# Weight tiles split into exact parts whole instead of in halves, in a two-block model's kernel

## The chip, the cores and the metric

The kernel runs on one core of a Trainium2 chip. The metric is the device time in microseconds of one execution. A profile of one execution lies beside the timed runs; its engines are named PE (TensorE's matmuls), PEld (TensorE's loads of the stationary operand), DVE (VectorE), ACT (ScalarE), POOL (GpSimd) and SP (SyncE, which issues most transfers).

## The reference: two model blocks in float32

The input is one sequence of 256 tokens of 1024 values, and a memory of 256 tokens. Block 1 is a token mixer (stick-breaking attention and a gated delta rule in chunks of 64), a cross attention to the memory, and a layer of product-key experts; block 2 is a second token mixer (gated linear attention and a spatial gating unit) and a second layer of experts. Each part is a norm, some dense layers `y = x @ w`, and something between them. The experts, which hold most of the weights, are

```python
def peer(xn, w_pq, subkeys, peer_u, peer_v):
    q = (xt @ w_pq).reshape(T, PEER_HEADS, 2, PEER_QDIM // 2)
    s = jnp.einsum('thpd,hpnd->thpn', q, subkeys)
    ...  # the 16 best of 128 x 128 sums of two scores per head: expert, gate
    def block(args):
        act = jax.nn.gelu(jnp.einsum('thkd,td->thk', peer_u[eb], xb), approximate=False) * gb
        return jnp.einsum('thk,thkd->td', act, peer_v[eb])
```

There are 16384 experts in each of the two layers. The kernel does not gather them: it multiplies every token with all rows of `peer_u` (the first layer of the experts), multiplies the activations by a dense matrix of gates that is zero where an expert was not chosen, and multiplies the result with all of `peer_v` (the second layer).

## The kernel before, in words

**Weights.** All weights come from memory in tiles of 128 x 1024 float32 values (512 KB). `load` (line 277) takes one of four `raw` buffers and issues the transfer from SP. `weight` (line 282) makes the two exact parts of a tile: `wh`, the values rounded to TensorE's float32r, and `wl`, what is left. Each part is made as two halves of 512 columns, with ScalarE's copy at line 274 for `wh` and VectorE's subtraction at line 275 for `wl`, both in `split`:

```python
    def split(self, hi, lo, src):
        self.nc.scalar.activation(hi, src, AF.Copy)
        self.nc.vector.tensor_tensor(lo, src, hi.bitcast(F32), ALU.subtract)
...
        raw = self.early.pop() if self.early else self.load(ap)
        wh, wl = [], []
        for i in range(2):
            wh.append(self.pw.tile([128, 512], F32R, tag="wh", bufs=HALF, name="wh"))
            wl.append(self.pw.tile([128, 512], F32R, tag="wl", bufs=HALF, name="wl"))
            self.split(wh[i], wl[i], raw[:, 512 * i:512 * i + 512])
        return Blocks(wh), Blocks(wl)
```

`HALF` is 7: there are seven half-size buffers for `wh` and seven for `wl`, so three and a half tiles. A half is written again when the matmuls that read it are done. The class `Blocks` gives the k-th block of 128 columns, or a whole half.

**Matmuls.** Each product is the sum of three: high by high, high by low and low by high (`mm3`, line 298, and the loops at lines 339 and 1265). In `dense` (line 301) a tile holds 128 output columns for all 1024 inputs, its eight blocks of 128 columns are the stationary operands in order, the tokens are the moving one (256 columns), and a tile takes 24 matmuls, twelve on each half. In `dense_tok` (line 326) and in the second layer of the experts (line 1265, `acc`) the half itself is the moving operand (512 columns); a tile takes twelve matmuls, six on the first half and then six on the second.

**Stages.** `mixer1`, `cross`, `peer`, `between`, `mixer2`, `peer`, `finish`, one after the other. In the mixers, `mix` weaves a chain of dependent steps (for instance `gdn`, the gated delta rule, with the triangular inverse by blocks of doubling size) with dense layers. In `peer` it weaves the selection of the experts (`route`, `gates`: sorting instructions and one-hot matrices on VectorE) with the first layer (`up`, `ph` in the profile). What is left of the first layer alternates with tiles of the second, and then the second layer goes on alone. For the second layer `prep` multiplies four rows of activations `hid` by gates `gt` that come by DMA (line 1209, VectorE) and splits the product into `dah` and `dal` (lines 274 and 275, ScalarE and VectorE).

**Order.** The tile framework puts the instructions of each engine into one order when the program is built, from the program's order and its own estimates of when operands and buffers are there. On the chip each engine takes its instructions strictly in that order, and waits where one is not ready.

There are 694 weight tiles in all, 512 of them in the two layers of experts.

Of the kernel before, what the change touches and what calls it, by code (L numbers as in the profile page):

```python
# [7 lines left out]
F32R = mybir.dt.float32r  # L8
# [10 lines left out]
T = 256  # L19
# [8 lines left out]
# pairs (a, b) of ranks that can be among the 16 best sums of two descending lists of 16: (a + 1) * (b + 1) <= 16, in  # L28
# the order of a * 16 + b; runs of equal length: first a, how many, length
RUNS = [(0, 1, 16), (1, 1, 8), (2, 1, 5), (3, 1, 4), (4, 1, 3), (5, 3, 2), (8, 8, 1)]  # L30
NC = 50
# blocks of q (0-3), k and v of the gated delta rule, in the order of their use
# [3 lines left out]
# ---------------------------------------------------------------- host layout  # L36
def _cols(w):
    """[K, C] -> [C/128, 128 p, K/128, 128 c]: one stationary tile per 128 columns."""
    k, c = w.shape
    return np.ascontiguousarray(w.reshape(k // 128, 128, c // 128, 128).transpose(2, 1, 0, 3))  # L40


def _rows(w):
    """[K, 512] -> [K/256, 128 p, 2, 512]: moving tiles, two blocks of 128 rows each."""
    k, c = w.shape
    return np.ascontiguousarray(w.reshape(k // 256, 2, 128, c).transpose(0, 2, 1, 3))


def _vec(v):
    """[n*128] -> [128, n]"""  # L50
    return np.ascontiguousarray(v.reshape(-1, 128).T)
# [107 lines left out]
# ---------------------------------------------------------------- the program  # L159
class Vec:  # L160
    """[128, n, 256] kept as tiles of four blocks"""
# [8 lines left out]
class Blocks:  # L170
    """[128, 1024] kept as two halves; [k] is the k-th block of 128 columns"""

    def __init__(self, half):
        self.half = half

    def __getitem__(self, k):
        return self.half[k // 4][:, k % 4 * 128:k % 4 * 128 + 128]
# [12 lines left out]
def weave(a, b):  # L190
    """steps of a and b by turns"""
    for _ in a:
        yield _
        v = next(b, None)
        if v is not None:
            yield v
    yield from b


def mix(a, b):  # L200
    """Two programs in one order. A step yields the vector engine's time that it takes, less what it leaves
    while the tensor engine is busy with it; a runs on what b leaves."""
# [16 lines left out]
class Norm:  # L219
    """x * g in exact halves (act), and the tokens' 1 / rms apart from it: rc with tokens on partitions, rb as rows.  # L220
    The latter are made when they are first asked for."""
# [12 lines left out]
class Net:  # L234
# [21 lines left out]
    # -- tiles  # L256
# [15 lines left out]
    # -- exact halves of float32: hi rounded to the tensor engine's float32r, lo the rest  # L272
# [9 lines left out]
    def weight(self, ap):  # L282
        """a tile [128, 1024] from memory: its exact parts, each as two halves"""
        raw = self.early.pop() if self.early else self.load(ap)
        wh, wl = [], []
        for i in range(2):
            wh.append(self.pw.tile([128, 512], F32R, tag="wh", bufs=HALF, name="wh"))
            wl.append(self.pw.tile([128, 512], F32R, tag="wl", bufs=HALF, name="wl"))
            self.split(wh[i], wl[i], raw[:, 512 * i:512 * i + 512])
        return Blocks(wh), Blocks(wl)  # L290

    def mm3(self, out, pairs):
        """sum of (ah+al)^T (bh+bl), without al^T bl, which is under float32's last place"""
# [7 lines left out]
    def dense(self, w, n, act, use):  # L301
        """w: tiles of 128 columns with K = 1024; use(pair, psum[128 c, 2 * 256 t])"""
# [11 lines left out]
    def dense_half(self, w, n, act, use):  # L314
        """w: tiles of two blocks of 128 columns with K = 512"""
# [10 lines left out]
    def dense_tok(self, w, act, use):  # L326
        """tokens on partitions: out[t, 512]; w: four moving tiles of two blocks of 128 rows; use(th, psum)"""
# [17 lines left out]
    def rsqrt(self, y, v, name):  # L345
        """y = v ** -0.5 for v > 0 on a few columns: a first value from the exponent, three Newton steps"""
# [14 lines left out]
    def spread(self, cols, n, out=None):  # L361
        """cols [128 t, n] -> the columns as rows on every partition: psum tiles of four [128, 128 t] each"""
# [12 lines left out]
    def begin(self, x, g, name, stats=True):  # L375
        """the norm of x[k] [128, 256] times g [128, 8], whose pairs of blocks are yet to be fed"""
# [51 lines left out]
    def colsum(self, ps, c, n, x):  # L428
        """ps[:, c] of n columns: the sums of x [128, 128 t] over its partitions"""
# [7 lines left out]
    def copies(self, v, N, scale=1.0):  # L437
        """use() that keeps pairs of column tiles in a Vec, times the tokens' 1 / rms"""
# [25 lines left out]
    def tables(self, which):  # L464
        """the activation tables that the calls of fn() after this one use, loaded after those before it are done"""
# [18 lines left out]
    # ------------------------------------------------------------ block 1, token mixer  # L484
    def sb_attention(self, qk, v, o):
        """stick-breaking; qk: Vec of 8 (4 of q / 8, 4 of k), two heads each; v [t][128, 512]; o: exact halves"""
# [4 lines left out]
        # scores, keys on partitions: of the first 128 keys all queries, of the others the last 128  # L491
# [17 lines left out]
        # softplus, which is zero where masked, and its sums over a key and those after it  # L509
# [24 lines left out]
    def gdn(self, pads, z, ba, out, ready):  # L534
        """gated delta rule; pads: 4 tiles [128, 3, 259] of q, k, v with three columns of zeros first;
        z [128 t, 2, 512]; ba [128 t, 2, 8] (b, then a); out: exact halves, Vecs of 4. ready: names of the blocks
        of pads, of ba and of z as they get there"""
# [17 lines left out]
        # beta, g, and the cumulative sums of g within chunks of 64  # L555
# [22 lines left out]
        gf = g.rearrange("p h c -> p (h c)")  # pack = 2 * head + half  # L578
# [13 lines left out]
        # l2 norms over the head's 128 partitions: k now, q with the output  # L592
# [18 lines left out]
        dm = self.big("dm", (8, 128))   # exp(gc_i - gc_j), i on partitions  # L611
        dt = self.big("dt", (8, 128))   # the same with j on partitions
        eg = self.big("eg", (8, 128))   # exp(gc) on every partition
# [8 lines left out]
        # of the differences d = gc_free - gc_partition only the signs that a causal pair can have  # L622
# [8 lines left out]
        # A, and q k^T with m on partitions  # L631
# [13 lines left out]
        # (I + A)^-1 by blocks of doubling size; Tm the inverse, P its transpose  # L645
# [11 lines left out]
        for s in (2, 4, 8, 16, 32):  # L657
# [25 lines left out]
            if s == 2:  # L683
                # meanwhile k and v with tokens on partitions, and q exp(gc)
# [14 lines left out]
        # u [c, dv] and w^T [dk, c]  # L699
# [11 lines left out]
        # the scan over chunks  # L711
# [38 lines left out]
    def head_out(self, po, th, z, g, out, rq=None, half=False):  # L750
        """the exact halves of rmsnorm(po * rq) * z * g for the heads' [128 t, 128], transposed; half: with z / 2"""
# [31 lines left out]
    def branches(self, gates, wa, oa, wb, ob, wout, N):  # L783
        """N: the norm of the new x.  x += (sigmoid(ga) * (oa @ wa) + sigmoid(gb) * (ob @ wb)) @ wout; gates: Vec of 16;
        sigmoid(y) = (tanh(y / 2) + 1) / 2"""
# [27 lines left out]
    def add_x(self, N):  # L813
        """use() that adds to x and feeds x's next norm"""
# [75 lines left out]
    # ------------------------------------------------------------ cross attention  # L890
# [23 lines left out]
    def patterns(self):  # L914
        """constants of the experts' selection, in 16 bits, which hold them"""
# [8 lines left out]
    def cross(self, N, kv):  # L924
# [54 lines left out]
        # the values of the last two heads, while the tensor engine has little else to do  # L979
# [10 lines left out]
    # ------------------------------------------------------------ product-key experts  # L990
    def peer(self, N, g, wpq, sub, shared, u, v, gelu, final):
        """returns psum tiles acc[t half][d half] of [128 t, 512] with x plus the experts' sums, and the tile of the
        final gain in rows"""
# [13 lines left out]
        # scores of half the heads and half the tokens each; later the gates on their way to memory  # L1007
# [11 lines left out]
        def scores():  # L1019
            """of the last head asked for; the tensor engine meanwhile has the next one's tiles"""  # L1020
# [14 lines left out]
        # of each selected expert: its two indices, and its gate times 2^15 in two parts of 11 bits  # L1035
# [4 lines left out]
        def route(hq, th):  # L1040
# [27 lines left out]
            # 64 * the first index + the place of the run, as steps from run to run  # L1068
# [41 lines left out]
            # the second index by its rank  # L1110
# [30 lines left out]
        def gates():  # L1141
            for t0 in range(0, T, 4):
# [3 lines left out]
                # one-hots of the first index; of the second, times each part of the gate  # L1146
# [54 lines left out]
        def prep(i0):  # L1201
            """gated activations of four rows of the table, in exact halves"""
# [29 lines left out]
        # the filler may reach the expert tables only after the normalized x is there  # L1232
# [5 lines left out]
        def tokens():  # L1238
            """adds x"""
# [9 lines left out]
        for i0 in range(0, 128, 4):  # L1249
# [3 lines left out]
            for i in range(4):  # L1253
                w[i] = self.weight(v[i0 + i])
                # the last two tiles go through the tokens' halves one after the other
# [11 lines left out]
                # what is left of the first layer, as the second one frees its place  # L1267
# [9 lines left out]
    def between(self, acc, gf):  # L1277
        """x <- rmsnorm(x + sums, g_final), and the next norm of it"""
# [26 lines left out]
        # the means of x^2 and (x g_final)^2, with eps; of the latter as the next norm has it, by the squared first rms  # L1305
# [48 lines left out]
    # ------------------------------------------------------------ block 2, token mixer  # L1354
    def mixer2(self, N):
# [5 lines left out]
        # the low rank and, on its own partition, a one for the bias  # L1361
# [168 lines left out]


class Rows:
    """the blocks of a [128, 8, 256] tile or Vec"""

    def __init__(self, x):
        self.x = x
# [31 lines left out]
```

## Time and profile before

| what | value |
|---|---|
| median of 3 runs | 2252.29 us (2251.95 to 2252.83) |
| span of the profiled execution | 2251.2 us |
| TensorE, matmuls | 2230.4 us busy, 99% of the span |
| VectorE | 1643.0 us, 73% |
| ScalarE | 1229.7 us, 55% |
| granted clock of TensorE, mean | 0.997 |
| read from memory, written | 403.89 MB, 34.60 MB |

The time of the profiled execution is its span; what lies around it is the 1.1 us to the runs' median. Busy time is the union of an engine's instructions. A matmul that waits for its operands can count as busy, so the numbers of matmuls in a stretch say more than its busy share. In a line of the page, `wl<-raw,wh 128x512 fp32r<-128x512 f32 x1388` is what an instruction writes and reads, its shapes and how often it ran; what stands in brackets or behind a bar is the idle time ahead of it and what ended that.

### The profile page before, as it was taken

The page shows a single profiled execution, that of the slowest core. Times are in us where ns is not written, and L with a number is a line of the kernel's source. Part 1 is how long each engine was busy: PE and PEld are TensorE (multiplying, and loading weights), DVE is VectorE, ACT ScalarE, POOL GpSimd, SP SyncE. Part 2 cuts the span into 40 slices and gives each one's busy share as a digit, 9 for nine tenths or more (in the row PEclk, how much of TensorE's full clock was granted, in tenths as well). Part 3 has the DMA queues.
Part 4 walks back from the last instruction along what each step waited for, and adds up shares of the span by engine and source line. Part 5 has one row for each costly group of instructions (what it writes and reads, how often), then busy time and mean ns, then how long its engine had stood idle before and what let it go on. Part 6 is the DMA issues. An engine that isn't in the chain of part 4 may idle for free.

```text
span 2251.2 us, 40741 instructions
## 1 busy us (share of the span) xinstructions
PE 2230.4 (99%) x15268; PEld 2035.2 (90%) x15268; DVE 1643.0 (73%) x3568; ACT 1229.7 (55%) x2237; POOL 1.8 (0%) x12
## 2 busy tenths in 40 slices
PE   8999999999999999999999999999999999999998
PEld 8899899999999999888887899999999999988886
DVE  8776776989778656687446668998887765598544
ACT  6463455656555555565446545655655555566443
POOL 0000000000000000000000000000000000000000
PEclk9999999999999999999999999999999999999999
DMA  6442445455666767787555445455566766698653
GB/s 232 139 150 85 132 150 178 161 189 178 208 231 216 243 206 221 232 288 251 188 188 189 143 132 186 156 192 186 202 217 213 247 216 207 214 297 262 200 190 125
DMA packets 178681, 441.14 MB, mean 196 GB/s; under 512 B 13602, under 2 KB 79266, under 8 KB 178484
## 3 DMA queue, kind: packets, MB, share of 16 engines
q1 hardware_dynamic: 177764, 437.11, 59.3%
q8 instruction: 120, 1.97, 0.4%
q10 hardware_dynamic: 720, 1.44, 0.2%
q14 instruction: 77, 0.63, 0.1%
HBM read 403.89 MB, written 34.60 MB: 195 GB/s over the span
## 4 chain that ended last, share of the span: by engine, by line
PE 95%; DVE 3%; ACT 1%; issue 1%; DMA 0%; ACTq 0%
PE ph L298 32%; PE acc L1265 32%; PE mm L298 17%; PE pg L1156 5%; PE mm L339 3%; DVE wl L275 1%; PE psc L1027 1%; ACT wh L274 0%; PE px L665 0%; PE pp L673 0%; PE cs L937 0%; PE pt L679 0%; PE cpo L963 0%; PE acc L1243 0%; PE spread L371 0%
## 5 line engine op out<-in xcount | busy, mean ns | idle before, releaser
L274 ACT ACTIVATE wh<-raw 128x512 fp32r<-128x512 f32 x1388 | 866.6, 630 | 853.5 <-PE ph L298 308.4
L275 DVE TENSOR_TENSOR wl<-raw,wh 128x512 fp32r<-128x512 f32 x1388 | 944.9, 688 | 483.4 <-ACT wh L274 477.2
L298 PE MATMUL ph<-pxh,wh 128*128 128x256 f32 x2048 | 579.4, 283 | 0.0
L298 PE MATMUL ph<-pxh,wl 128*128 128x256 f32 x2048 | 571.9, 279 | 0.0
L298 PE MATMUL ph<-pxl,wh 128*128 128x256 f32 x2048 | 571.4, 279 | 0.0
L1265 PE MATMUL acc<-wh,dah 128*128 128x512 f32 x1024 | 405.5, 396 | 0.0
L1265 PE MATMUL acc<-wh,dal 128*128 128x512 f32 x1024 | 405.0, 396 | 0.0
L1265 PE MATMUL acc<-wl,dah 128*128 128x512 f32 x1024 | 405.0, 396 | 0.0
L298 PEld LDWEIGHTS ph<-pxh,wh 128*128 128x128 f32 x2048 | 386.5, 189 | 3.1
L298 PEld LDWEIGHTS ph<-pxl,wh 128*128 128x128 f32 x2048 | 385.5, 188 | 3.2
L298 PEld LDWEIGHTS ph<-pxh,wl 128*128 128x128 f32 x2048 | 384.8, 188 | 0.0
L1265 PEld LDWEIGHTS acc<-wh,dal 128*128 128x128 f32 x1024 | 192.3, 188 | 46.6
L1265 PEld LDWEIGHTS acc<-wh,dah 128*128 128x128 f32 x1024 | 192.4, 188 | 43.0
L1265 PEld LDWEIGHTS acc<-wl,dah 128*128 128x128 f32 x1024 | 192.4, 188 | 42.9
L298 PE MATMUL mm<-xnh,wh 128*128 128x256 f32 x496 | 142.7, 288 | 8.9 <-ACT wh L274 8.1
L298 PE MATMUL mm<-xnh,wl 128*128 128x256 f32 x496 | 141.4, 285 | 0.0
L298 PE MATMUL mm<-xnl,wh 128*128 128x256 f32 x496 | 140.7, 284 | 0.0
L1156 PE MATMUL pg<-work 128*128 128x128 f16 x1024 | 133.3, 297 | 0.0
L1156 PEld LDWEIGHTS <-work 128*128 128x128 f16 x1024 | 110.3, 118 | 4.5
L1209 DVE TENSOR_TENSOR hid<-hid,gt 128x512 f32<-128x512 f32 x128 | 86.0, 688 | 35.9 <-DMA gt<-gd 35.2
L274 ACT ACTIVATE dah<-hid 128x512 fp32r<-128x512 f32 x128 | 76.3, 621 | 61.9 <-DVE hid L1209 60.9
L298 PEld LDWEIGHTS mm<-xnh,wh 128*128 128x128 f32 x496 | 95.2, 192 | 11.2 <-ACT wh L274 8.1
(443 smaller groups left out, 2825.7 us busy)
## 6 DMA issues: line engine op xcount, KB each, us to landing
raw<-in_u_dram SPq DMA_DIRECT2D x256, 512.0 KB, 3.6
raw<-in_v_dram SPq DMA_DIRECT2D x256, 512.0 KB, 3.9
gd<-S SPq DMA_DIRECT2D x64, 512.0 KB, 4.1
gt<-gd SPq DMA_DIRECT2D x64, 512.0 KB, 5.8
raw<-in_w_gate_dram SPq DMA_DIRECT2D x32, 512.0 KB, 3.5
raw<-in_w_pq_dram SPq DMA_DIRECT2D x32, 512.0 KB, 3.5
raw<-in_w_g_dram SPq DMA_DIRECT2D x12, 512.0 KB, 4.7
raw<-in_w_qk_dram SPq DMA_DIRECT2D x8, 512.0 KB, 3.5
```

Source lines behind the costliest of these rows:

```text
L274: self.nc.scalar.activation(hi, src, AF.Copy)
L275: self.nc.vector.tensor_tensor(lo, src, hi.bitcast(F32), ALU.subtract)
L298: self.nc.tensor.matmul(out, l, r, start=i == 0, stop=i == n - 1)
L339: nc.tensor.matmul(ps[th], l, r, start=k == 0 and j == 0, stop=k == 7 and j == 2)
L1027: nc.tensor.matmul(pz[:, p * 128:p * 128 + 128], qf[:, p * 256 + th * 128:p * 256 + th * 128 + 128], key(h, p), start=True, stop=True)
L1156: nc.tensor.matmul(pg[:, t * 128:t * 128 + 128], hot[:, c, :, t], hot[:, 0, :, t], start=c == 2, stop=c == 3)
L1209: tt(hv, hv, gv, ALU.mult)
L1265: nc.tensor.matmul(acc[th][dh], l[:, n, sl], r.half[dh], start=i0 + n == 0 and j == 0, stop=i0 + n == 127 and j == 2)
```

## The change

Each part of a tile becomes one buffer of 1024 columns, made by one operation of ScalarE and one of VectorE. There are three such buffers for `wh` and three for `wl`, so three tiles in place of three and a half. Nothing else of the program is changed: `Blocks` gives the same blocks and halves as slices of the whole tile. (Comments and empty lines also differ; they are left out here.)

```diff
 class Blocks:
-    def __init__(self, half):
-        self.half = half
+    def __init__(self, t):
+        self.t = t
+        self.half = [t[:, 0:512], t[:, 512:1024]]
 
     def __getitem__(self, k):
-        return self.half[k // 4][:, k % 4 * 128:k % 4 * 128 + 128]
+        return self.t[:, k * 128:k * 128 + 128]
...
     def weight(self, ap):
         raw = self.early.pop() if self.early else self.load(ap)
-        wh, wl = [], []
-        for i in range(2):
-            wh.append(self.pw.tile([128, 512], F32R, tag="wh", bufs=HALF, name="wh"))
-            wl.append(self.pw.tile([128, 512], F32R, tag="wl", bufs=HALF, name="wl"))
-            self.split(wh[i], wl[i], raw[:, 512 * i:512 * i + 512])
+        wh = self.pw.tile([128, 1024], F32R, tag="wh", bufs=PARTS, name="wh")
+        wl = self.pw.tile([128, 1024], F32R, tag="wl", bufs=PARTS, name="wl")
+        self.split(wh, wl, raw)
         return Blocks(wh), Blocks(wl)
...
-RAW, HALF = 4, 7
+RAW, PARTS = 4, 3
```

## Rows read from the trace of the kernel before

**Rows 1.** The page: busy us per engine, and the chain that ended last by engine.

```profile
PE 2230.4 (99%) x15268; PEld 2035.2 (90%) x15268; DVE 1643.0 (73%) x3568; ACT 1229.7 (55%) x2237; POOL 1.8 (0%) x12
...
PE 95%; DVE 3%; ACT 1%; issue 1%; DMA 0%; ACTq 0%
```

**Rows 2.** Stretches: us, length, busy us (instructions) per engine, clock, DMA share, GB/s.

```profile
1450.00:1500.00 50.00, 50.00 (x431) 50.00 (x430) 49.97 (x214) 27.43 (x47) 0.00 (x0) 1.00 0.51 170
1000.00:1050.00 50.00, 50.00 (x233) 40.99 (x232) 43.41 (x73) 27.63 (x52) 0.00 (x0) 1.00 0.83 264
1100.00:1150.00 50.00, 50.00 (x216) 40.26 (x215) 24.55 (x36) 22.79 (x36) 1.07 (x3) 1.00 0.59 188
```

**Rows 3.** Waits of the whole span: us in total, times, longest us.

```profile
DVE wl L275 <- ACT wh L274: 477.2, 666, 2.8
ACT wh L274 <- PE ph L298: 308.4, 458, 0.8
...
PE mm L298 <- ACT wh L274: 8.1, 1, 8.1
```

**Rows 4.** Timeline of the quiet stretch: start us, us, engine, operation.

```profile
1101.31 0.40 PE L1265 MATMUL acc<-wh,dal 128*128 128x512 f32 x1
1101.74 0.63 ACT L274 ACTIVATE wh<-raw 128x512 fp32r<-128x512 f32 x1 [0.77 <-PE acc L1265]
1102.40 0.69 DVE L275 TENSOR_TENSOR wl<-raw,wh 128x512 fp32r<-128x512 f32 x1 [0.71 <-ACT wh L274]
1110.17 0.40 PE L1265 MATMUL acc<-wl,dah 128*128 128x512 f32 x1
```

**Rows 5.** Groups by line and shape: busy us, mean ns, idle before.

```profile
L275 DVE TENSOR_TENSOR wl<-raw,wh 128x512 fp32r<-128x512 f32 x1388 | 944.9, 688 | 483.4 <-ACT wh L274 477.2 <-PE mm L298 1.0
L274 ACT ACTIVATE wh<-raw 128x512 fp32r<-128x512 f32 x1388 | 866.6, 630 | 853.5 <-PE ph L298 308.4 <-PE acc L1265 268.4 <-PE mm L298 189.5
L479 ACT ACTIVATE hid<-ph 128x512 f32<-128x512 f32 x128 | 74.5, 582 | 0.1
L1098 DVE TENSOR_TENSOR work<-work,rdw 128x1024 f32<-128x1024 bf16 x8 | 9.7, 1214 | 0.0
L479 ACT ACTIVATE gate<-gate 128x1024 f32<-128x1024 f32 x8 | 8.3, 1056 | 1.7 <-DVE gate L448 1.7
```

**Rows 6.** Timeline in the second layer of block 1, near 1050 us.

```profile
1047.06 1.16 ACT L274 ACTIVATE dah<-hid 128x512 fp32r<-128x512 f32 x2 [4.06 <-DVE hid L1209]
1049.69 3.74 ACT L274 ACTIVATE wh<-raw 128x512 fp32r<-128x512 f32 x7
1051.10 4.30 DVE L275 TENSOR_TENSOR wl<-raw,wh 128x512 fp32r<-128x512 f32 x7
1052.77 0.40 PE L1265 MATMUL acc<-wl,dah 128*128 128x512 f32 x1
```

**Rows 7.** Timeline of the start, ScalarE, VectorE and TensorE's loads.

```profile
7.42 1.13 ACT L274 ACTIVATE wh<-raw 128x512 fp32r<-128x512 f32 x2
8.07 1.29 DVE L275 TENSOR_TENSOR wl<-raw,wh 128x512 fp32r<-128x512 f32 x2
8.81 0.29 PEld L298 LDWEIGHTS mm<-xnh,wl 128*128 128x128 f32 x1 [0.22 <-DVE wl L275]
```

**Rows 8.** Timeline of the selection: the first and the last of eight dips.

```profile
440.61 4.29 DVE L275 TENSOR_TENSOR wl<-raw,wh 128x512 fp32r<-128x512 f32 x7
443.03 0.28 PE L298 MATMUL ph<-pxh,wl 128*128 128x256 f32 x1
1590.48 1.29 DVE L275 TENSOR_TENSOR wl<-raw,wh 128x512 fp32r<-128x512 f32 x2
1593.87 0.28 PE L298 MATMUL ph<-pxh,wl 128*128 128x256 f32 x1
```

**Rows 9.** Timeline in the second layer of block 2, near 2085 us.

```profile
2081.69 4.49 DVE L275 TENSOR_TENSOR wl<-raw,wh 128x512 fp32r<-128x512 f32 x7
2084.86 0.40 PE L1265 MATMUL acc<-wl,dah 128*128 128x512 f32 x1
```

## The prediction

> **What bounds the kernel now.** I read the page's busy times first [rows 1]: TensorE is busy 2230.4 of 2251.2 us, VectorE 73% and ScalarE 55%. The chain that ended last gives TensorE 95%. Busy matmuls can hide waiting, so the table by stretch [rows 2] comes next, and there the reader should look at the counts. From 1450 to 1500 us TensorE issues 431 matmuls of 256 columns, 0.116 us apart; a tile has 24 of them, so 2.8 us. From 1100 to 1150 us it issues 216 of 512 columns, 0.23 us apart, 12 to a tile: 2.8 us again. Two very different loads of VectorE (49.97 and 24.55 of 50 us) leave TensorE at its pace. So the path is TensorE's, and the other engines matter only when a weight part comes after TensorE has asked for it. Today that never lasts: in the table of waits [rows 3] TensorE's one long wait for a part is the 8.1 us at the start. The long waits run the other way: VectorE waits 477.2 us for wh, ScalarE 308.4 us for buffers that the matmuls of line 298 hold. The parts run ahead as far as their buffers allow.
>
> The view that decides is therefore the timeline of one part, from the release of its buffer to its first use: how much time is to spare, and how much is left after the change.
>
> **The reserve, before and after.** Take the quiet stretch [rows 4]. The last matmul on a half starts at 1101.31, the next half begins at 1101.54, and ScalarE refills the freed buffer from 1101.74, 0.20 us after that boundary. VectorE follows at 1102.40 and ends at 1103.09. With seven buffers this part is taken six halves after 1101.54, 6 x 1.4 = 8.4 us, at 1109.94, and its wl at 1110.17. From finished to needed: 7.08 us. That is the reserve with halves.
>
> With three whole buffers a tile is released when the next one begins, call it T. ScalarE starts at T + 0.20. No 1024-wide copy of this kind is in the trace; the nearest is line 479 on 128x1024 from and to SBUF, 1056 ns [rows 5]. Bounds: 1056 below, and two halves in a row above, about 0.63 + 0.52 = 1.15 us (seven take 3.74 us, so they start 0.52 apart [rows 6]). I take 1.06: ready at T + 1.26. VectorE starts 0.03 later as now (1102.37 to 1102.40). For its 1024-wide operation the nearest row is line 1098, 1214 ns for 1024 float32 results [rows 5]; above it stand two halves in a row, 1.29 us (seven in 4.30 us, 0.60 apart [rows 6]). I take 1.22: done at T + 2.51. The tile is taken two tiles later, its wl at T + 5.60 + 0.23 = T + 5.83. Reserve 3.32 us. **The change takes 3.76 us of reserve away.** Half a tile less buffering is only a part of this; the rest is that nothing is released in the middle of a tile and nothing handed on before the whole tile is done.
>
> **What it gives.** 694 tiles save, on VectorE, 1.29 - 1.22 = 0.07 us each where halves stand in a row (up to 2 x 0.688 - 1.214 = 0.16 where they stand alone): 49 us of a 73% busy engine. ScalarE saves 1.15 - 1.06 = 0.09 us each, 62 us of a 55% busy engine. I cost both at nothing on the path: TensorE's 2.8 us per tile covers them. They count only while VectorE is behind.
>
> The Trainium skill, Perfetto Trace Analysis, section Optimizing Scalar/DVE Operations, says both things: grouping into larger operations helps if the engine is saturated, with about 60 ns (DVE) and 93 ns (Scalar) of overhead per SBUF instruction, and breaking operations up may help where these engines are not saturated but make others wait. By its figures, as an estimate, 694 fewer operations on each are worth 42 and 65 us of engine time, near the sums from rows; by its second half the change is the wrong way round.
>
> **Where the smaller reserve does not do.** I followed the 1388 wl parts [rows 5] against the halves TensorE takes, matched by order, and looked for places where finished-to-needed falls below 3.76 us.
>
> *Start* [rows 7]. ScalarE starts on wh at 7.42, VectorE on wl at 8.07, and TensorE takes the first wl at 8.81 after waiting for it. Whole: 7.42 + 1.06 = 8.48, then 8.51 + 1.22 = 9.73. That is 0.9 us later, with nothing before it to hide it.
>
> *Selection of experts beside the first layer*, about 425 to 600 and 1457 to 1610 us. VectorE falls behind the route's steps eight times. The first and the last of the eight [rows 8]: wl done at 440.61 + 0.68 = 441.29 and taken at 443.03, 1.74 us; done at 1591.16, taken at 1593.87, 2.71 us. All eight: 1.74, 2.89, 2.52, 2.73, then 2.53, 2.86, 2.54, 2.71, sum 20.5. While it falls behind, over some 7 tiles, the wider operations give 7 x 0.07 = 0.5 us back. A dip of S costs 3.76 - 0.5 - S; the eight cost 8 x 3.26 - 20.5 = 5.6 us. Between dips the reserve is full again, so each counts by itself.
>
> *Second layer with the gates' rows arriving*. ScalarE sits 4.06 us in front of dah until VectorE has multiplied hid, which waits for its DMA; all wh copies queue behind it. Afterwards it makes seven wh without one wait on TensorE, so all seven buffers stood empty; wl is done at 1051.10 + 0.69 and taken at 1052.77, 0.98 us [rows 6]. The same happens smaller twice: 2.23 us near 1021 and, the last, 2084.86 - (2081.69 + 0.69) = 2.48 us [rows 9]. Relief here 3 tiles, 0.2: 3 x 3.56 - 5.7 = 5.0 us.
>
> Everywhere else the distance is above 3.76 us or within half a microsecond of it, most of all in the quiet stretches: nothing.
>
> **Sum.** 0.9 + 5.6 + 5.0 = 11.5 us on a span of 2251.2; the runs' median lies 1.1 above that span, so 2252.3 + 11.5 = 2263.8 us, 0.5% slower.
>
> Bounds. Above: no relief (8 x 0.5 + 3 x 0.2 = 4.6), and in the first layer ScalarE's activation of hid, 582 ns [rows 5], which is released by the same tile end as the next wh and now always stands before it (8 x 0.58 = 4.6): 2273. Below: only the start, 2253.
>
> **Rivals.**
> *The dips move or shrink*: about no change. The order on each engine is made anew from the program by the tile framework; wl and other steps need not meet as they do now, and the dips are made by such meetings (dah and wl alternate on VectorE near 1050). Against it: the same steps with the same priority and less buffering. With the start and a quarter of the dips: 0.9 + 2.7, 2256.
> *Dependent chains get longer*: slower still. In the first mixer the triangular inverse of the gated delta rule makes 28 dependent steps on VectorE (five sizes, two groups, three results, but for the last size's two). Each may find a whole subtraction in front of it, 1.22 instead of 0.69. If all do and TensorE has nothing else, 28 x 0.53 = 15 us more, 2279. Against: TensorE has other tiles there.
> *VectorE is the real limit*: faster. It is full from 1450 to 1500 us [rows 2], and 0.07 us per tile frees it. It decides only where TensorE waits for VectorE, and of TensorE's 20.8 idle us [rows 1] 8.1 are the start, before any part exists, and most of the rest the tail after the last matmul. At most some 5 us: 2247. Beside it stands the first half of the Trainium skill's rule named above, which the full VectorE of this stretch would call for.
>
> **How the numbers follow.** Less than 0.2% (4.5 us) can hardly be told from no change here. Pauses at the dips, the forecast: 0.60, own range 2257 to 2273. Dips shrink: 0.25. Longer chains: 0.10. VectorE's relief: 0.05. So slower 0.70, same 0.25, faster 0.05. The range of 8 in 10 runs from 2252 to 2279: below lie the faster case and a little of "same".
>
> **What would show it.** wh and wl at 1024 wide, 694 each, near 1.06 and 1.22 us; VectorE's busy time between 1531 and 1594 us (0.16 or 0.07 per tile), ScalarE's between 1088 and 1168. In the quiet stretch nothing but the operations changes: still 216 matmuls in 50 us. The first wl is taken near 9.7 us. Fewer matmuls per 50 us near 443, 522, 1021, 1053 and 2085 than now, with TensorE released there by wl. The forecast is wrong if TensorE keeps its counts in those stretches (dips shrank), if the loss is in the first 300 us instead (chains), or if losses appear in every tile (then the reserve of 3.32 us was misjudged).

## The result, and the profile after

The kernel after takes 2264.53 us (median of 4 runs, 2263.73 to 2266.01), the kernel before beside it 2252.56 us (4 runs, 2251.95 to 2255.14). The ratio is 1.0053, 95% interval 1.0038 to 1.0067: 12.0 us slower by the medians, 0.5%. The profiled execution has a span of 2262.0 us, 10.8 more than before. The forecast of 2263.8 us and its sign held. Its parts held less well, as the stages below show.

First the page of the kernel after: busy us per engine, the chain that ended last, and the two groups that the change made. `wh` now stands at line 275 and `wl` at line 276; the lines behind `split` and `weight` moved the other way (298 is now 297, 1265 now 1264).

```profile
PE 2236.3 (99%) x15268; PEld 2037.2 (90%) x15268; DVE 1566.5 (69%) x2874; ACT 1101.1 (49%) x1543; POOL 1.8 (0%) x12
...
PE 88%; DVE 8%; DMA 2%; ACT 1%; issue 1%; SPq 0%; ACTq 0%; DVEq 0%
...
L275 ACT ACTIVATE wh<-raw 128x1024 fp32r<-128x1024 f32 x694 | 735.1, 1060 | 1029.9 <-PE ph L297 393.2
L276 DVE TENSOR_TENSOR wl<-raw,wh 128x1024 fp32r<-128x1024 f32 x694 | 845.9, 1221 | 445.7 <-ACT wh L275 444.6
```

Both operations cost what the nearest rows said: 1.06 and 1.22 us. VectorE is busy 76.5 us less than before and ScalarE 128.6 us less [rows 1], both within the bounds of the prediction, and the kernel is slower. TensorE's busy time grew by 6 us for the same 15268 matmuls, which is waiting that counts as busy. In the chain TensorE's share fell from 95% to 88%, VectorE's rose from 3% to 8%.

The reserve can be read off the timeline of the quiet stretch (start us, us, engine, line, operation).

```profile
1101.66 0.40 PE L1264 MATMUL acc<-wh,dal 128*128 128x512 f32 x1
1101.89 0.40 PE L1264 MATMUL acc<-wh,dah 128*128 128x512 f32 x1
...
1102.09 1.06 ACT L275 ACTIVATE wh<-raw 128x1024 fp32r<-128x1024 f32 x1 [1.74 <-PE acc L1264]
...
1103.19 1.22 DVE L276 TENSOR_TENSOR wl<-raw,wh 128x1024 fp32r<-128x1024 f32 x1 [1.58 <-ACT wh L275]
...
1107.73 0.40 PE L1264 MATMUL acc<-wl,dah 128*128 128x512 f32 x1
```

The next tile begins at T = 1101.89. ScalarE starts 0.20 us later, `wl` is done at 1104.41, T + 2.52, and is taken at 1107.73: 3.32 us of reserve, the number of the forecast. Nothing waits here. That shows in the table by stretch as well (length, busy us with instructions per engine, clock, DMA share, GB/s):

```profile
400.00:450.00 50.00, 49.33 (x422) 48.92 (x422) 46.89 (x202) 28.21 (x43) 0.00 (x0) 1.00 0.52 165
450.00:500.00 50.00, 49.96 (x424) 49.49 (x423) 42.00 (x119) 22.61 (x26) 0.00 (x0) 1.00 0.57 185
500.00:550.00 50.00, 50.00 (x428) 49.82 (x428) 44.00 (x165) 26.44 (x33) 0.00 (x0) 1.00 0.57 179
...
1000.00:1050.00 50.00, 50.00 (x232) 40.76 (x231) 42.89 (x56) 26.93 (x36) 0.00 (x0) 1.00 0.89 278
...
1100.00:1150.00 50.00, 50.00 (x216) 40.24 (x215) 22.03 (x18) 18.68 (x19) 1.07 (x3) 1.00 0.58 189
...
1450.00:1500.00 50.00, 49.24 (x420) 48.84 (x420) 47.82 (x204) 24.07 (x33) 0.00 (x0) 1.00 0.51 168
```

Read the counts against [rows 2]. The quiet stretch still has 216 matmuls. The stretch at 1000 us, where a loss was forecast, has 232 after 233. The selection at 1450 us has 420 after 431: 11 matmuls of 0.116 us, 1.3 us in this one stretch. At 500 us the busy share is a full 50.00 and three matmuls are missing (431 before): only the count tells.

What TensorE waits for is in the table of waits (us in total, times, longest). Line 297 is `mm3` in the first layer (`ph`) and in dense layers (`mm`), line 1264 the second layer.

```profile
PE mm L297 <- ACT wh L275: 8.4, 1, 8.4
...
PEld ph L297 <- DVE wl L276: 4.3, 9, 0.9
...
PEld mm L297 <- DVE wl L276: 2.1, 3, 0.8
...
PEld acc L1264 <- DVE wl L276: 1.9, 4, 0.9
```

Waits for `wl` were next to nothing before; now TensorE's loads have 16, of 0.5 us on average. One of them, at the first dip of [rows 8] (two and a half tiles ahead of the part shown there):

```profile
438.10 1.22 DVE L276 TENSOR_TENSOR wl<-raw,wh 128x1024 fp32r<-128x1024 f32 x1
438.50 1.05 ACT L275 ACTIVATE wh<-raw 128x1024 fp32r<-128x1024 f32 x1
...
439.37 0.39 PE L297 MATMUL ph<-pxh,wl 128*128 128x256 f32 x1 [0.62 <-DVE wl L276]
```

VectorE came to this `wl` late from its sorting steps and ended at 439.32. TensorE's matmul before began at 438.47, so at 0.12 us a matmul this one was due at 438.59; it began at 439.37, 0.8 us late. (The 0.62 us in the row count from the end of the matmul before.)

**Where the time goes, by stage.** I took the start of the same matmul (counted by its kind) in two traces; the difference is the delay so far, and how it grows from stage to stage is the loss of each. Each stage ends at a mark; in the times of before these are 427, 627, 933, 1211, 1459, 1659, 1965 and 2243 us (the last matmul).

| kernel | reserve, us | start, mixer 1, cross | selection 1 | rest of first layer | second layer 1 | mixer 2 | selection 2 | rest | second layer 2 | sum |
|---|---|---|---|---|---|---|---|---|---|---|
| after | 3.32 | 2.6 | 3.2 | 0.1 | 0.1 | 0.5 | 3.2 | -0.1 | 1.1 | 10.7 |
| e1, 6 halves | 5.68 | 0.7 | 0.0 | 0.1 | 5.2 | 0.6 | 0.0 | 0.7 | 1.0 | 8.2 |
| e2, 5 halves | 4.28 | -0.5 | 2.0 | 0.1 | 1.8 | 0.0 | 1.1 | -0.1 | 4.1 | 8.4 |
| e3, 4 halves | 2.88 | 4.0 | 7.2 | 0.0 | 8.9 | 0.9 | 6.3 | 0.0 | 3.6 | 30.9 |
| e4, 4 whole | 6.12 | 1.6 | 0.0 | 0.0 | 0.0 | -2.4 | 0.0 | 0.0 | 0.0 | -0.8 |
| e5, 3 whole by halves | 4.28 | 0.2 | 2.4 | 0.0 | 5.9 | -1.4 | 1.1 | 0.0 | 11.6 | 19.8 |
| e6, 2 whole | 0.52 | 13.9 | 12.4 | 3.2 | 3.6 | 9.0 | 12.4 | 3.4 | 3.8 | 61.7 |
| e8, 6 halves, early gates | 5.68 | 0.3 | 0.1 | 0.1 | 0.0 | -0.2 | 0.0 | 0.0 | 0.0 | 0.3 |
| e9, 3 whole, early gates | 3.32 | 2.8 | 3.4 | 1.3 | 4.3 | -0.7 | 3.2 | 1.4 | 2.2 | 17.8 |
| e10, e5 with early gates | 4.28 | -0.1 | 2.3 | 0.1 | 6.4 | -1.1 | 1.3 | 0.0 | 0.0 | 8.9 |
| e11, 4 whole, early gates | 6.12 | 1.9 | 0.0 | 0.0 | 0.1 | -0.6 | 0.0 | 0.0 | 0.5 | 1.9 |
| e12, 7 halves, early gates | 7.08 | 0.9 | 0.1 | 0.1 | 2.2 | -1.5 | 0.0 | 0.0 | 2.4 | 4.1 |

The reserve of each kernel is worked out as in the prediction: 1.4 us less for each half-size buffer fewer, 2.8 us more or less for each whole one. The rows e1 to e12 belong to the experiments; e7 isn't in the table, since its order of matmuls differs.

### The profile page after: what moved, and what is told of

It is laid out like the page before. It is cut to its first block, busy times and chain, and to the rows that moved or that the text cites. A ratio compares the mean times of both kernels' runs of the same rounds, so it can differ in the third digit from the quotient of the medians.

```text
span 2262.0 us, 38322 instructions
## 1 busy us (share of the span) xinstructions
PE 2236.3 (99%) x15268; PEld 2037.2 (90%) x15268; DVE 1566.5 (69%) x2874; ACT 1101.1 (49%) x1543; POOL 1.8 (0%) x12
## 4 chain that ended last, share of the span: by engine, by line
PE 88%; DVE 8%; DMA 2%; ACT 1%; issue 1%; SPq 0%; ACTq 0%; DVEq 0%
PE ph L297 29%; PE acc L1264 28%; PE mm L297 16%; PE pg L1155 5%; PE mm L338 4%; DVE wl L276 3%; DMA gt<-gd 2%; ACT wh L275 1%; DVE scr L1049 0%; PE px L664 0%; PE pp L672 0%; DVE ti L1051 0%; PE psc L1026 0%; DVE dal L276 0%; DVE tv L1050 0%
## 5 line engine op out<-in xcount | busy, mean ns | idle before, releaser
L275 ACT ACTIVATE wh<-raw 128x1024 fp32r<-128x1024 f32 x694 | 735.1, 1060 | 1029.9 <-PE ph L297 393.2
L276 DVE TENSOR_TENSOR wl<-raw,wh 128x1024 fp32r<-128x1024 f32 x694 | 845.9, 1221 | 445.7 <-ACT wh L275 444.6
L1147 DVE TENSOR_TENSOR work<-iota,ids 128x1024 f16<-128x1024 f16 x128 | 88.6, 692 | 79.8 <-PE pg L1155 79.8
```

Of the source, the lines that this page charges most:

```text
L1147: tt(hot[:, 0:2], self.iota4.unsqueeze(1).broadcast_to([128, 2, 128, 4]), ids[:, :, t0:t0 + 4].unsqueeze(2).broadcast_to([128, 2, 128, 4]) ...
```

## The experiments

**The number of half-size buffers, alone: e1, e2, e3.** The theory: the reserve sets the pauses, so the kernel before loses in the same places if it only has fewer halves.

```diff
-RAW, HALF = 4, 7
+RAW, HALF = 4, 6     # e2: 5, e3: 4
```

> Halves as before, six buffers per part instead of seven: the same 24 KB per partition for each pair of parts as three whole tiles. Reserve theory: 7.08 - 1.40 = 5.68 us, so only a part that now comes under 1.4 us before its use (one, at 0.98) can make TensorE wait: at most +0.4 us, 2252 to 2254, the same within 0.2%. Rival (it is the half tile less buffering that costs): about the changed kernel's time, 2262 to 2265. Rival (the planner's new order costs, whatever the reserve): any new order may cost, some +5 us or more.

> Halves, five buffers per part. Reserve theory: 7.08 - 2.80 = 4.28 us, 2.80 lost. Selection beside the first layer: sum of 2.80 - S over the dips of 1.74, 2.52, 2.73, 2.53, 2.54, 2.71 us = 2.0 us; second layer 0.6 + 0.3, and up to 1.8 for the dip of 0.98, which cost nothing in the changed kernel: +2.5 to +4.7 us, 2255 to 2257. No relief of VectorE in it. Rival (order): no relation to the number of buffers.

> Halves, four buffers per part, two tiles. Reserve theory: 7.08 - 4.20 = 2.88 us, 0.44 less than with three whole tiles, and no relief of VectorE: selection 8 x 4.20 - 20.5 = 13.1 us, second layer about 1 to 3, mixers some 2 as in the changed kernel: +15 to +19 us, 2267 to 2272, so slower than the changed kernel although no operation is wide. Rival (the width of the operations costs, not the reserve): at or under the changed kernel's time. Rival (order): no relation.

Beside 2253.3 us of before (2252.26 to 2255.69, 20 runs) they took 2261.03 us (ratio 1.0033, 1.0021 to 1.0045), 2261.69 us (1.0033, 1.0023 to 1.0043) and 2282.55 us (1.0127, 1.0112 to 1.0143). All three are slower than their expected range. In the two selections the theory did well: 0.0 us for e1, 3.1 for e2 (2.0 expected), 13.5 for e3 (13.1 expected). In the second layers it failed: e1 lost 6.2 us there where at most 0.4 was expected, e2 5.9 for at most 2.7, e3 12.5 for 1 to 3. The waits of e1 from 940 to 1100 us, and below them those of before in the same stretch, say where:

```profile
ACT dah L274 <- DVE hid L1209: 41.3, 13, 5.5
...
DVE hid L1209 <- DMA gt<-gd: 19.1, 13, 3.5
...
PEld acc L1265 <- DVE wl L275: 6.9, 10, 1.6
```

```profile
ACT dah L274 <- DVE hid L1209: 33.8, 13, 4.6
...
DVE hid L1209 <- DMA gt<-gd: 13.8, 9, 3.6
```

The third wait isn't there before. VectorE stands in front of `hid` until the gates `gt` land, ScalarE in front of `dah` until `hid` is done, and the next part of a tile is queued behind both. Where the tile framework puts these steps is planned anew for each kernel.

**Four whole buffers: e4.** Wide operations with a large reserve, so that width and reserve come apart.

```diff
-RAW, PARTS = 4, 3
+RAW, PARTS = 4, 4
```

> The changed kernel with four whole buffers per part instead of three. Reserve theory: 3.32 + 2.80 = 6.12 us, 0.96 lost against halves, less than every dip but none: the pauses go, the start's 0.9 us stays: 2253 to 2254. Rival (width of the operations costs): still 2262 or more. Rival (relief of VectorE is worth something once the reserve is there): under 2250, faster than before.

Selections and second layers lose nothing with 1024-wide operations. So the width isn't what costs there; and no stage got faster by VectorE's relief. (The second mixer's 2.4 us less isn't a sign of it: e12, with the operations of before, has 1.5 us less there.) The start keeps its part of the loss. The runs' median is 2256.26 us (2252.39 to 2257.61, 11 runs), ratio 1.0013, 1.0004 to 1.0022, against 2253 to 2254 expected. The table's row is that of the fastest of them, with a span of 2250.5 us; the others' spans lie between 2252.3 and 2255.7 us, and where those spend it isn't recorded. e11 below, another kernel with four whole buffers, loses nothing in its selections either.

**Whole buffers filled by halves: e5.** After's three buffers, each written by two half-size operations per engine. The first half of a part is done at T + 0.20 + 0.63 + 0.03 + 0.69, so the reserve is 4.28 us, that of e2, with operations of the same size as in e2.

```diff
-        self.split(wh, wl, raw)
+        for i in range(2):
+            sl = slice(512 * i, 512 * i + 512)
+            self.split(wh[:, sl], wl[:, sl], raw[:, sl])
```

> The changed kernel's three whole buffers, released whole, but each filled by two half-size operations per part instead of one. Reserve theory: the first half of wl is done at T + 0.20 + 0.63 + 0.03 + 0.69 = T + 1.55, so the reserve is 4.28 us, that of five halves: the two selections together lose 2 to 3 us by the profile (6.4 in the changed kernel, 3.1 with five halves), the start 0 instead of 0.9; the second layers as the new order has it, 0 to 6. In all 2255 to 2262. Rival (only the half tile less buffering and the release in whole tiles cost): the selections lose 6.4 as in the changed kernel. Rival (only the width costs): they lose nothing.

2269.5 us (2267.06 to 2273.32), ratio 1.0071, 1.0057 to 1.0085, beside 2253.81 us of before: slower than the kernel after, and than the 2262 us expected at most. The selections lost 3.5 us, near e2's 3.1 at the same reserve and half of after's 6.4 at the smaller one. The start lost nothing: TensorE takes the first `wl` at 8.68 us, against 9.67 in after (second line) and 8.81 before [rows 7]. Nearly all of the rest, 17.5 us, is in the second layers.

```profile
8.68 0.28 PEld L299 LDWEIGHTS mm<-xnh,wl 128*128 128x128 f32 x1 [0.22 <-DVE wl L276]
```

```profile
9.67 0.29 PEld L297 LDWEIGHTS mm<-xnh,wl 128*128 128x128 f32 x1 [0.76 <-DVE wl L276]
```

**Two whole buffers: e6.**

```diff
-RAW, PARTS = 4, 3
+RAW, PARTS = 4, 2
```

> The changed kernel with two whole buffers per part. Reserve theory: 3.32 - 2.80 = 0.52 us, 6.56 lost against halves: the two selections 8 x (6.56 - 0.5) - 20.5 = 28 us, the second layers about 13, every activation of hid in front of a wh (0.58 against 0.52) a little, the mixers some 10 and more: 2300 to 2330. The long quiet stretches of the second layers still lose nothing, 216 matmuls in 50 us. Rival (the order costs, not the reserve): near 2264.

2315.04 us (2312.28 to 2316.16), ratio 1.0269, 1.0254 to 1.0285. The selections lost 24.8 us (28 expected), the second layers 7.4 (about 13 expected), the start and the mixers 22.9 (some 10 and more). The table by stretch shows it at 400 us (395 matmuls, 432 before), and the quiet stretch even at 0.52 us of reserve untouched (216, as before):

```profile
400.00:450.00 50.00, 46.86 (x395) 46.00 (x394) 48.16 (x228) 27.68 (x45) 0.00 (x0) 1.00 0.43 140
...
1100.00:1150.00 50.00, 50.00 (x216) 40.26 (x215) 21.67 (x19) 19.08 (x18) 1.07 (x3) 1.00 0.56 186
```

**Less of VectorE's time beside each tile: e7.** `mix` weaves a step of the first layer in for each 1.4 us of the selection's steps on VectorE; with 1.2 there are more tiles beside the selection.

```diff
-    UP = 1.4
+    UP = 1.2
```

> The changed kernel with the constant UP at 1.2 instead of 1.4: the weaving gives the selection 0.2 us less of VectorE per weight tile of the first layer, so VectorE falls behind less while the reserve stays 3.32 us. Reserve theory (a pause is VectorE's lag beyond the reserve): the selections' 6.4 us of pauses go down to 0 to 2, in all 2257 to 2261 if the second layers and mixers stay. Rival (the wide operations or their order cost, not the lag): the selections keep their 6.4 us.

Not as expected: 2305.67 us (2301.47 to 2309.8), ratio 1.0227, 1.0213 to 1.0241. In the first selection TensorE's waits for `wl` are the same 2.2 us in five pieces as in after, so nothing was gained, and the first layer's tiles that may run ahead of the second layer are used up before the selection is done. TensorE then waits for it (waits of the whole span, and one stretch):

```profile
PEld acc L1264 <- ACT dah L275: 18.8, 2, 9.5
```

```profile
765.00:770.00 5.00, 2.41 (x20) 2.13 (x21) 4.15 (x7) 1.83 (x6) 0.00 (x0) 0.50 0.52 201
770.00:775.00 5.00, 2.82 (x23) 2.25 (x21) 1.88 (x4) 2.96 (x8) 0.00 (x0) 0.50 0.68 229
775.00:780.00 5.00, 0.00 (x0) 0.00 (x0) 0.99 (x2) 0.00 (x0) 0.00 (x0) 0.50 0.81 288
```

**The gates' transfer started four rows earlier: e8.** If late gates are what costs in the second layers, their earlier start should cure e1.

```diff
-            if i0 % 8 == 4 and i0 + 4 < 128:
-                fetch(i0 + 4)
+            if i0 % 8 == 0 and i0 + 8 < 128:
+                fetch(i0 + 8)
```

> Six half buffers per part as in the first experiment, with the gates' rows asked for four rows of the table earlier (at the first instead of the second prep of a group of eight). That experiment lost 6.2 us in the two second layers and nothing in the selections. Theory (VectorE waits for gt in front of hid, ScalarE in front of dah, and wh queues behind it): VectorE's waits for gt go from some 19 us near 1000 us to under 8 and the second layers' loss to under 2: 2253 to 2256. Rival (the order of the preps itself, too close together): the loss stays at 5 or more while the waits for gt go.

2254.29 us (2252.19 to 2256.94, 11 runs), ratio 1.0003, 0.9994 to 1.0012: all of e1's loss is gone. From 940 to 1100 us VectorE still waits 11.1 us for `gt`, where under 8 was expected, and no `dah` of ScalarE's waits for `hid` in that stretch:

```profile
DVE hid L1209 <- DMA gt<-gd: 11.1, 9, 2.6
```

But the edit did not only start the transfers earlier. Set against TensorE's matmuls, the transfers of the two stretches 940 to 1100 and 1970 to 2130 us start 12.1 and 8.3 us earlier than in e1 (medians), and the `hid` steps that use them come 10.3 and 7.0 us earlier as well: the framework planned both anew. So the gates gained little lead, and whether that or the new order cured e1 isn't shown by this run.

**The same edit in four other kernels: e9 to e12.** In after, in e5, in e4 and in before. Before on this chip took 2253.23 us (21 runs).

> The kernel after with one edit: the gates' transfer of eight table rows is started when row i0 is prepared instead of four rows later, as in e8. It computes the reference. Theory (the reserve of split parts sets the selections, late gates and the planner's order set the second layers): the selections keep their 6.4 us, the start and the mixers keep theirs (about 0.9 and 2), and of the second layers' 1.2 us most goes: 2262 to 2264 us, about 1 below the kernel after. Rival (the second layers lose because wide operations hold VectorE and ScalarE longer, whatever the gates do): unchanged within 0.5 us. A second rival (gates' earlier transfers collide with raw tiles' loads): over 1 us slower than the kernel after.

> e5 (three whole buffers, each filled by two half-size operations) with the gates started four rows earlier. It computes the reference. Theory: e5's 17.5 us in the two second layers came from gates that landed late and held VectorE and ScalarE in front of the next split, so they go, and the selections' 3.5 us and about 1 us elsewhere stay: 2255 to 2259 us. Rival (two half-size operations for one whole buffer are by themselves what loses there): stays over 2265.

> e4 (four whole buffers per part) with the gates started four rows earlier. It computes the reference. Theory: a reserve of 6.12 us leaves the selections free, and the second layers lost nothing in e4's profiled run, so 2252 to 2255 us; if the 4 us between e4's runs came from gates that land late in some of them, this kernel's runs lie closer together, within 2 us. Rival (the spread has nothing to do with the gates): runs from 2252 to 2257 as in e4.

> The kernel before with the gates started four rows earlier, nothing else changed. It computes the reference. Theory: before has hardly a pause for gates on TensorE's path, so within 2 us of before, 2251 to 2254; it says what the earlier gates give by themselves. Rival (the planner's order gets worse or transfers collide): over 2255.

All four levels were missed, to the slow side: 2270.82 us (ratio 1.0075, 1.0062 to 1.0089), 2262.13 us (1.0043, 1.0030 to 1.0057), 2257.29 us (1.0019, 1.0010 to 1.0028) and 2256.39 us (1.0012, 1.0003 to 1.0021). So an earlier start is no cure by itself. In e9 the second layers lose more than in after (6.5 against 1.2 us), and before itself gets 4.5 us of loss there in e12, with next to no wait of ScalarE for `hid` (1.3 and 2.3 us). In e10 the second layer of block 2 goes from 11.6 us to nothing, that of block 1 stays. Within e9 the path of one pause is plain in the timeline:

```profile
986.47 1.29 DVE L1208 TENSOR_TENSOR hid<-hid,gt 128x512 f32<-128x512 f32 x2 [2.07 <-DMA gt<-gd]
...
987.85 0.63 ACT L275 ACTIVATE dah<-hid 128x512 fp32r<-128x512 f32 x1 [2.50 <-DVE hid L1208]
...
988.82 2.08 DVE L276 TENSOR_TENSOR dal<-hid,dah 128x512 fp32r<-128x512 f32 x3
...
990.82 1.22 DVE L276 TENSOR_TENSOR wl<-raw,wh 128x1024 fp32r<-128x1024 f32 x1
...
992.09 0.19 PEld L1264 LDWEIGHTS acc<-wl,dah 128*128 128x128 f32 x1 [0.51 <-DVE wl L276]
```

VectorE stands 2.07 us until the gates come, `hid` twice and `dal` three times go first, and the `wl` that TensorE's pace wants at 991.85 us (its matmul before starts at 991.62) is done at 992.04. Here are the waits of e9 from 940 to 1100 us, and those of e12 in the same stretch below them:

```profile
DVE hid L1208 <- DMA gt<-gd: 15.6, 11, 2.1
ACT dah L275 <- DVE hid L1208: 13.6, 7, 2.9
...
PEld acc L1264 <- DVE wl L276: 6.0, 10, 1.3
```

```profile
DVE hid L1209 <- DMA gt<-gd: 18.9, 11, 2.6
...
PEld acc L1265 <- DVE wl L275: 3.0, 5, 1.1
```

With the earlier start e12's VectorE waits longer for `gt` than before's does (18.9 against 13.8 us): the framework put `hid` earlier as well. By the medians used for e8, taken in the two stretches, it did so in each of these kernels:

| kernel, beside | transfer earlier, us | `hid` earlier, us |
|---|---|---|
| e8, e1 | 12.1, 8.3 | 10.3, 7.0 |
| e9, after | 16.0, 15.7 | 16.0, 16.6 |
| e10, e5 | 10.2, 14.1 | 10.3, 14.1 |
| e11, e4 | 12.1, 13.6 | 11.3, 14.2 |
| e12, before | 11.2, 10.0 | 9.8, 8.6 |

The edit moves the transfer and its use together, so these runs don't test a longer lead of the gates. What can be read is how the loss of a second layer goes with VectorE's wait for `gt` in its stretch (940 to 1100 or 1970 to 2130 us), over all kernels but e7:

| buffers per part | wait for `gt`, us: loss, us |
|---|---|
| seven halves | 10.9: 0, 13.8: 0, 18.9: 2.2, 18.9: 2.4 |
| six halves | 9.7: 0, 11.1: 0, 12.3: 1.0, 19.1: 5.2 |
| five halves | 13.3: 1.8, 15.6: 4.1 |
| four halves | 12.8: 3.6, 20.5: 8.9 |
| three whole, by halves | 10.3: 0, 16.7: 6.4, 18.2: 5.9, 24.0: 11.6 |
| four whole | 13.3: 0, 14.3: 0.1, 15.5: 0.5, 20.1: 0 |
| three whole | 13.5: 0.1, 14.4: 2.2, 15.6: 4.3, 17.0: 1.1 |
| two whole | 7.9: 3.6, 10.3: 3.8 |

Among kernels with the same buffers the loss goes up with the wait, nearly in order, but not with three or four whole buffers; and seven halves lose 2.2 us at 18.9 us of wait where four whole ones, with less reserve, lose nothing at 20.1. So much of the loss goes with the wait for the gates, and single pauses can be followed back to it; that the wait makes all of the loss isn't shown, and a single figure for it doesn't price it.

The spread of e4's runs wasn't narrowed either: e11's go from 2254.71 to 2260.15 us.

## Why the prediction was right, and where its parts were not

*The reserve* (7.08 us with halves, 3.32 us whole) was right to the hundredth, and it is what the selections depend on most. Ordered by reserve, the kernels' two selections together lost 0.0 (6.12), 0.0 (5.68), 3.1 and 3.5 (4.28), 6.4 (3.32), 13.5 (2.88) and 24.8 us (0.52), kernels with operations of 512 and of 1024 columns in one order; e9 (3.32) and e10 (4.28) repeat it with 6.5 and 3.6. e5 beside e2, the same operations at the same reserve, shows that whole buffers do nothing of their own there; e4 beside after, that a fourth buffer with the same operations takes all 6.4 us away.

If the width of the operations counts in the selections, it is as a gain. Without the 0.5 us of relief at each dip, the prediction's sum gives 8 x 3.76 - 20.5 = 9.6 us for after and 8 x 6.56 - 20.5 = 32 us for e6; they lost 6.4 and 24.8. e3, with half-size operations and no relief in its sum, lost 13.5 for 13.1. That fits the relief that the prediction counted while VectorE is behind, some 3 us in after. No two runs differ in the width alone at one reserve, so this rests on the sums and isn't shown by itself.

*The eight selection dips*, 5.6 us forecast, cost 6.4. The first selection's four sum to 3.16 by the formula 3.26 - S (3.2 measured), the second's to 2.4 (3.2 measured). One by one the dips were not met: the first was forecast at 3.26 - 1.74 = 1.52 us, and over it the delay grew by 1.25; the second at 0.37 (0.8 measured), the first of the second selection at 0.73 (1.3 measured). So the mechanism and the size of the sum were right, and errors of single dips cancel in it.

*The start*, 0.9 us forecast: the first `wl` is taken at 9.67 us instead of 8.81. e5, with the same buffers filled by halves, takes it at 8.68, so here it is the width that costs. This is the place to come back to the rule weighed in the prediction, the Trainium skill, Perfetto Trace Analysis, section Optimizing Scalar/DVE Operations. Its half on breaking operations up agrees with this case at the start. Its half on grouping holds for the engine (1.22 against 1.29 us for two halves in a row); by the sums above it takes some of the loss off where VectorE is full, in the dips, and it makes no stage faster than before, as e4 shows.

*The second-layer dips*, 5.0 us forecast, cost 1.2. **This term was mis-sized**, by the assumption under it that the order on VectorE and ScalarE stays as it is: the place near 1050 us alone was to cost 3.56 - 0.98 = 2.58 us and cost nothing [rows 6]. ScalarE's waits for `hid` from 940 to 1100 us fell from 33.8 to 15.7 us in after:

```profile
ACT dah L275 <- DVE hid L1208: 15.7, 9, 3.3
```

The steps meet differently there, since the framework planned them anew. That was the rival of the dips that move. It came true for one of the two groups of dips, while the other kept its places. What is left is mostly one pause near 2057 us (0.75 of the 1.1 us in that layer), well ahead of the place near 2085 us that was forecast [rows 9]:

```profile
2054.49 1.29 DVE L1208 TENSOR_TENSOR hid<-hid,gt 128x512 f32<-128x512 f32 x2 [1.75 <-DMA gt<-gd]
...
2055.21 1.15 ACT L275 ACTIVATE dah<-hid 128x512 fp32r<-128x512 f32 x2 [3.46 <-DVE hid L1208]
...
2055.70 1.22 DVE L276 TENSOR_TENSOR wl<-raw,wh 128x1024 fp32r<-128x1024 f32 x1
...
2056.97 0.49 PE L1264 MATMUL acc<-wl,dah 128*128 128x512 f32 x1 [0.49 <-DVE wl L276]
```

*The mixers*, put at nothing beyond the start, cost 1.7 of the first stage's 2.6 us and 0.5 in the second mixer. One pause of 0.6 us is seen at 282.23 us, where VectorE makes `mgl`'s two halves and a step of `gate` before a `wl`:

```profile
279.16 1.28 DVE L806 SCALAR_TENSOR_TENSOR mgl<-gate,mgh 128x512 fp32r<-128x512 f32 x2
280.96 1.22 DVE L276 TENSOR_TENSOR wl<-raw,wh 128x1024 fp32r<-128x1024 f32 x1
...
282.23 0.38 PE L297 MATMUL mm<-mgh,wl 128*128 128x256 f32 x1 [0.45 <-DVE wl L276]
```

An equal one stands in the second mixer, at 1392.84 us. The prediction put these places at nothing because no distance fell more than half a microsecond below 3.76 us there; where the other 1.1 us of the first stage went wasn't followed.

The rival of the longer dependent chains, 15 us, didn't come: before the cross attention ended the delay was 2.6 us in all. Nor did the rival of VectorE as the real limit: 76.5 us less busy, and no stage of after clearly faster than before.

So 3.8 us less in the second layers and 0.8 + 2.2 us more in the selections and mixers nearly cancel: 0.9 + 6.4 + 1.2 + 2.2 = 10.7 us of span, where 11.5 was forecast. That the total is within 1 us of the median is partly luck: the term of the second layers ranged over the kernels from 0 to 17.5 us.

**What stays open.** Why the framework's order leaves the gates late in one kernel and not in the next can't be read from a trace; only that it does. How much of the second layers' loss the wait for the gates makes, and how much the order of the other steps, is open too, since every edit here changed both. The runs of e4 and e11 lie above their profiled ones by a few microseconds, and what differs wasn't seen, since only one of each was recorded in full. No kernel here beats the one before; e8 equals it with a half tile's buffer less.

## What to carry to other kernels

Before merging operations, measure the reserve of what they make: the time from finished to first used, at steady pace and at the worst dip. Merging and cutting buffers takes from it what release and handing-on in the middle gave, and each dip then costs what was taken, less the reserve that the dip had left before. That sum can be trusted where the order of work around the dip is likely to stay (the selections, within 15% in after, e3 and e6; e2 lost 3.1 us for 2.0); where a framework plans the order anew, take the other kernels' spread as the error, not the one trace. And that an engine has become less busy proves nothing by itself: look for what waits for it, and when.

## What the runs showed of the hardware that was not expected

In e7, TensorE's granted clock fell while it was short of work: from 1.00 in the stretch from 745 to 750 us, where it issued 36 matmuls, to between 0.76 and 0.89 in the three stretches of 5 us after it and 0.50 from 765 to 785 us, the lower of its two levels (1.2 GHz). It issued 31, 34, 27, 20 and 23 matmuls in the five stretches before it stopped altogether, and after work came back it was at 0.82 from 785 to 790 us and 1.00 from 790. So the waits of 18.8 us for `dah` came with slow matmuls around them: at 752.84 to 754.12 us those of 256 columns start 0.21 us apart, where 0.116 is their regular pace. TensorE's waits of up to 1.2 us for `wl` in the first layers of after, e3 and e6 left the clock at 1.00 in every 50 us of theirs that I looked at.
